# A mixture-of-experts stage on TensorE: which products share the four column tiles, and which engine turns the hidden activations

## The chip, the cores and the metric

One core of a Trainium2 chip runs the program. The metric is device time in microseconds (us), from launch to end, as the median of repeated executions; a profiled execution gives the trace. TensorE is called PE below, its weight loads PEld, VectorE DVE, ScalarE ACT, and SP is the queue that issues the transfers.

## What is computed

A sequence of 256 tokens of width 1024, in fp32, goes through a convolution layer with a dense feed-forward part, a sliding-window attention layer with a mixture of experts, two hybrid layers and a last norm. The change touches the mixture alone:

```python
def moe_swiglu(h, router, we_gate, we_up, we_down):
    logits = (h @ router).astype(jnp.float32)
    top_v, top_i = lax.top_k(logits, TOP_K)
    top_w = jax.nn.softmax(top_v, axis=-1)
    gates = jnp.sum(jax.nn.one_hot(top_i, N_EXPERTS) * top_w[..., None], axis=-2)
    out = jnp.zeros_like(h)
    for e in range(N_EXPERTS):
        out = out + gates[..., e:e + 1] * swiglu(h, we_gate[e], we_up[e], we_down[e])
    return out
```

There are 8 experts and each token goes to 2 of them. An expert has two matrices of 1024 x 3584 (gate and up) and one of 3584 x 1024 (down), 44 MB in fp32, 352 MB for all eight.

## The kernel before

**Slots.** Each expert works on its own tokens only. They are gathered into 96 slots (`CAP`), three blocks of 32 (blocks 0 to 2). `prepare` (L1404) makes ready two experts at a time: `onehot` (L1321) builds the token-to-slot matrix on DVE, `gather` (L1334) multiplies the normed tokens with it (32 matmuls), and `back` (L1354) turns it for the way back. `back` makes, for one expert, 6 transposes of 128x128 on PE, 6 products of 128x1 (the gate of every slot), each of which appears as two instructions, and masked copies on ACT. Were an expert to have more than 96 tokens, a second pass would run (L1315); it does not run in this execution.

**Products.** A matmul whose stationary operand has 32 columns fills one of four column tiles of the array, and its result goes to 32 partitions of a PSUM bank; four such matmuls, one per tile, run at the same time (`four`, L1417). An fp32 matmul appears as two instructions in the trace. The stationary operand is a block of 32 slots, the moving one 256 columns of weights. The hidden width of 3584 is cut into 14 chunks of 256. In `proj` (L1422) tiles 0 to 2 hold the three slot blocks and stream the same chunk of weights; tile 3 takes one of the blocks with another chunk, so that four chunks make three steps. An expert has 9 such steps and one for its last two chunks. The four matmuls of a group thus stream two different pieces of weights. The down products (`down`, L1477) do the same with four column parts of the down weights.

**Between the two products.** `act` (L1447) makes silu(gate) * up on ACT and DVE, 128 partitions x 256. `turn` (L1465) transposes it on PE, two transposes of 128x128 (four of 96x96 in the last step), into a PSUM bank, from which DVE copies it. `finish` (L1488) calls `turn`, then the down products. The loop (L1506) issues the projections of step n and then finishes step n-1, so the transposes stand between two runs of expert products on PE.

**Way back.** After an expert's last step `scatter` (L1380) splits its three partial outputs into a high and a low part, scaled by the slots' gates (ACT, then DVE), and multiplies them with the turned one-hot matrices (24 matmuls of 128x256 in all, as the fourth column part is spread over the blocks); DVE adds the result into `xT`, the running residual.

**Order.** All calls are recorded and a planner (`Recorder.issue`, L541) lays out a fixed order for each engine and assigns buffers, by estimated costs; an instruction that would wait in the plan lets a later one pass. All instructions therefore carry one line in the trace, L685. Weight tiles of 512 KB go to `large` buffers (35, at most 33 for raw weights) by transfers on SP, in the order of the program, each as soon as a buffer is free: 84 per expert. PSUM has 8 banks. `MEM_AT` and `GATHER_AT` (L44, L45) say before or after which step two other pieces of work go in: the memory keys and values of the second hybrid layer (`mem_second`), at step 22 of 80, and `prepare` for the next two experts, after the fourth step of every second expert. After the mixture the kernel reads a count into a register and branches (L1314 to L1316), and the next layer begins.

Of the kernel before, what the change touches and what calls it, by code (L numbers as in the profile page):

```python
# [30 lines left out]
NC4 = 3  # L31
# [12 lines left out]
MEM_AT = 2, 122  # L44
GATHER_AT = 1, 0  # L45
# [38 lines left out]
def _ch(w):  # L84

    return w.reshape(2, 4, 128, w.shape[1] // 256, 256).transpose(3, 2, 0, 1, 4)
# [49 lines left out]
def _consts():  # L136
# [37 lines left out]
    add("slot", np.broadcast_to((np.arange(2 * CAP) % CAP)[None, :] - BIG, (128, 2 * CAP)))  # L174
    add("part", np.concatenate([p < CAP, p >= CAP], 1))
# [16 lines left out]
def layout(i):  # L192
# [21 lines left out]
        "e_gate": np.stack([_ch(w) for w in i["sw_we_gate"][0]]),  # L214
        "e_up": np.stack([_ch(w) for w in i["sw_we_up"][0]]),
        "e_down": np.stack([_dn(w) for w in i["sw_we_down"][0]]),
# [471 lines left out]
class Net:  # L688
# [632 lines left out]
    def onehot(self, e, base):  # L1321

        nc = self.nc
        both = [self.t([128, 2, 2 * CAP], F32R, "onehot") for _ in range(2)]
        for j in range(2):
            for i in range(2):
                at = self.pos[:, j, e + i:e + i + 1]
                if base:
                    nc.vector.tensor_scalar(both[j][:, i], self.C("slot"), base, at, op0=OP.add, op1=OP.is_equal)
                else:  # L1330
                    nc.vector.tensor_scalar(both[j][:, i], self.C("slot"), at, None, op0=OP.is_equal)
        return both

    def gather(self, oh):  # L1334
        nc = self.nc
        G = [[], []]
        for c in range(4):
# [4 lines left out]
            for i in range(2):  # L1342
                at = (2 * c + i) % 4 * 128
                for n in range(4):
                    part, j = n // 2, n % 2
                    nc.tensor.matmul(pv[:, i], self.xn[j][part][c // 2][:, at:at + 128], oh[j][:, :, :CAP],
                                     start=n == 0 and i == 0, stop=n == 3, skip_group_check=True)
# [6 lines left out]
    def back(self, oh, x, e):  # L1354

        nc = self.nc
        pa, pb = self.acc("pmt"), self.acc("pmt")
        for v in range(3):
            p, at = (pa, v * S) if v < 2 else (pb, 0)
            for j in range(2):  # L1360
                nc.tensor.transpose(p[:, at + j * 128:at + (j + 1) * 128], oh[j][:, x, 32 * v:32 * v + 128].bitcast(F32),
                                    self.C("ident"))
        for v in range(3):
            for j in range(2):
                nc.tensor.matmul(pb[:, S + v:S + v + 1], oh[j][:, x, 32 * v:32 * v + 128].bitcast(F32),
                                 self.gate[:, j, e:e + 1], start=j == 0, stop=j == 1, skip_group_check=True)
        T = []
        low, high = self.C("part", 0, 1), self.C("part", 1, 1)
        two = [self.t([128, 2, S], F32R, "ohT") for _ in range(2)]
        for t, m in zip(two, (low, high)):  # L1370
            nc.scalar.activation(t.rearrange("p a s -> p (a s)"), pa, AF.Copy, scale=m)
        one = self.t([128, 2, S], F32R, "ohT")
        for n, m in enumerate((low, high)):
            nc.scalar.activation(one[:, n], pb[:, :S], AF.Copy, scale=m)
        gs = self.sm(3, "gs")
        nc.vector.tensor_copy(gs, pb[:, S:S + 3])
        T = [(two[0][:, 0], two[1][:, 0]), (two[0][:, 1], two[1][:, 1]), (one[:, 0], one[:, 1])]
        return T, gs

    def scatter(self, back, y):  # L1380
        nc = self.nc
        T, gs = back
        ys = []
        for v in range(3):
            h = self.t([128, S], F32R, "yh")
            l = self.t([128, S], F32R, "yl")
            self.split(h, l, y[v], scale=gs[:, v:v + 1])
            ys.append((h, l))
        for mp in range(4):
            p = self.acc("psc")  # L1390
            todo = [(v, part) for v in ([mp] if mp < 3 else range(3)) for part in range(2)]
            for i in range(2):
                for n, (v, part) in enumerate(todo):
                    nc.tensor.matmul(p[:, i * S:(i + 1) * S], ys[v][part][:, i * 128:(i + 1) * 128], T[v][mp == 3],
                                     start=n == 0 and i == 0, stop=n == len(todo) - 1, skip_group_check=True)
            nc.vector.tensor_tensor(self.xT[mp], self.xT[mp], p.rearrange("p (a s) -> p a s", a=2), op=OP.add)

    def experts(self, base=0.0):
        nc, a = self.nc, self.a
        steps = [(e, q, v) for e in range(NE) for q in range(NC4) for v in range(3)]  # L1400
        steps = [s for e in range(NE) for s in [x for x in steps if x[0] == e] + [(e, NC4, 0)]]
        G, B, Y, H, T, D = {}, {}, {}, {}, {}, {}
# [8 lines left out]
        def chunk(name, e, c):  # L1411
            return self.load_raw(a[name][e, c])

        def rows(e, k, b):
            return G[e][k][:, 32 * b:32 * b + 32]

        def four(outs, x, w, start, stop):  # L1417

            for j in range(4):
                nc.tensor.matmul(outs[j], x[j], w[j], start=start, stop=stop, skip_group_check=True)  # L1420

        def proj(s):  # L1422
            e, q, v = s
            p = self.mm()
            quarter = lambda p, at: [p[32 * j:32 * j + 32, at:at + 256] for j in range(4)]
            if q < NC4:
                if v == 0:
                    D[e, q] = [chunk(n, e, 4 * q + 3) for n in ("e_gate", "e_up")]
                mine = [chunk(n, e, 4 * q + v) for n in ("e_gate", "e_up")]
                for k in range(KT):  # L1430
                    u, i = k // 4, k % 4
                    x = [rows(e, k, j if j < 3 else v) for j in range(4)]
                    for m in range(2):
                        ws = [mine[m][u][:, i]] * 3 + [D[e, q][m][u][:, i]]
                        four(quarter(p, m * 256), x, ws, k == 0 and m == 0, k == KT - 1)
                return p
            last = [chunk(n, e, c) for n, c in (("e_up", 13), ("e_gate", 12), ("e_up", 12), ("e_gate", 13))]
            p2 = self.mm()
            for m in range(3):
                out = quarter(p if m < 2 else p2, m % 2 * 256)  # L1440
                for k in range(KT):
                    u, i = k // 4, k % 4
                    x = [rows(e, k, j if j < 3 else m) for j in range(4)]
                    four(out, x, [last[1 + m][u][:, i]] * 3 + [last[0][u][:, i]], k == 0 and m != 1, k == KT - 1)
            return p, p2

        def act(s, p):  # L1447
            e, q, v = s
            if q < NC4:
                g = self.t([128, 256], F32, "eg")  # L1450
                nc.scalar.activation(g, p[:, :256], AF.Silu)
                nc.vector.tensor_tensor(g, p[:, 256:], g, op=OP.mult)
                H[s] = [g]
                return
            p, p2 = p
            g, h = self.t([128, 256], F32, "eg"), self.t([128, 256], F32, "eg")
            nc.scalar.activation(g[:CAP], p[:CAP, :256], AF.Silu)
            nc.vector.tensor_tensor(g[:CAP], p[:CAP, 256:], g[:CAP], op=OP.mult)
            nc.scalar.activation(h[:CAP], p2[:CAP, :256], AF.Silu)
            for b, up in enumerate((p[96:, :256], p[96:, 256:], p2[96:, :256])):  # L1460
                r = slice(32 * b, 32 * b + 32)
                nc.vector.tensor_tensor(h[r], up, h[r], op=OP.mult)
            H[s] = [g, h]

        def turn(s):  # L1465
            n = 128 if s[1] < NC4 else CAP
            hs = H.pop(s)
            pt = self.acc("pht")
            t = self.t([128, 2 * len(hs), n], F32, "eh")
            pv = pt[:, :2 * len(hs) * n].rearrange("p (a b) -> p a b", b=n)  # L1470
            for x, g in enumerate(hs):
                for i in range(2):
                    nc.tensor.transpose(pv[:, 2 * x + i], g[:n, i * 128:(i + 1) * 128], self.C("ident")[:n, :n])
            nc.vector.tensor_copy(t, pv)
            T[s] = t

        def down(e, c, cols):  # L1477
            if c == 0:
                y = [self.acc("y0"), self.acc("y1")]
                Y[e] = [y[0][:, :256], y[0][:, 256:], y[1][:, :256]]  # L1480
            for i, w in enumerate(self.load_raw(a["e_down"][e, c])):
                for v in range(3):
# [250 lines left out]
```

## Time and profile before

| what | value |
|---|---|
| median of 3 runs | 2251.2 us (2250.46 to 2252.23) |
| profiled execution | 2245.66 us |
| its span | 2243.8 us |
| mean granted clock of TensorE | 0.987 |
| moved by DMA | 556.93 MB, mean 248 GB/s |

The span is what the trace covers; the profiled execution's time is 1.9 us longer. The trace gives, for any stretch of the span, each engine's busy time, its instructions in order of time, who waited for whom, and the rate of the DMA engines. Matmul ends are modelled, so where matmuls follow one another the pace is read from the starts.

### The profile page before, as it was taken

To read this page: it belongs to the slowest core of one execution; us is meant where nothing else is said; L and a number is where in the kernel's file an instruction comes from. 1 tells how busy PE (TensorE), PEld (TensorE's weight loads), DVE (VectorE), ACT (ScalarE), POOL (GpSimd) and SP (SyncE) were. 2 spreads that over 40 slices of the span, in tenths; PEclk is the share of its full clock that TensorE was granted. 3 is DMA by queue.
4 is the path that set the end of the run, shared out by engine and by line. 5 is a ranking of instruction groups with operands and counts; after the bars stand their busy time and mean duration, and the time that the engine had idled before them with its cause. 6 is when DMAs were issued, how large, how long until landed. Compare 5 with 4: busy or idle time off the path is not lost. (4 is left out here: it accounts for less than half of the span.)

```text
span 2243.8 us, 58323 instructions
## 1 busy us (share of the span) xinstructions
PE 2197.1 (98%) x25832; PEld 1716.0 (76%) x25832; DVE 917.3 (41%) x1911; ACT 717.0 (32%) x1259; POOL 0.2 (0%) x4
## 2 busy tenths in 40 slices
PE   8999999999999999999999999899999999999998
PEld 8789997865656556555665555487999998799997
DVE  8976568401101010010101010275485566657554
ACT  9454457310100001000010000165454454545441
POOL 0000000000000000000000000000000000000000
PEclk9999999999999999999999999998999999999998
DMA  7345657389889998999989999282466555355550
GB/s 281 92 160 174 202 186 247 132 315 384 335 303 342 352 401 304 388 379 400 334 319 375 399 358 376 72 333 69 125 222 192 186 180 188 102 163 178 189 169 20
DMA packets 156221, 556.93 MB, mean 248 GB/s; under 512 B 17456, under 2 KB 20144, under 8 KB 155952
## 3 DMA queue, kind: packets, MB, share of 16 engines
q1 hardware_dynamic: 155952, 553.03, 69.2%
q8 instruction: 206, 3.38, 0.6%
q14 instruction: 63, 0.52, 0.1%
HBM read 551.92 MB, written 1.05 MB: 246 GB/s over the span
## 5 line engine op out<-in xcount | busy, mean ns | idle before, releaser
L685 PE MATMUL bank<-large,gen 128*32 128x256 f32 (+2 forms) x15092 | 1006.4, 379 | 11.3 <-ACT gen L685 8.8
L685 PE MATMUL bank<-gen,large 128*128 128x256 f32 x7524 | 931.8, 285 | 8.1 <-ACT large L685 7.2
L685 PEld LDWEIGHTS bank<-gen,large 128*128 128x128 f32 x7524 | 910.2, 189 | 23.5 <-ACT large L685 7.6
L685 PEld LDWEIGHTS bank<-large,gen 128*32 128x32 f32 (+1 forms) x15092 | 612.9, 115 | 350.6 <-ACT gen L685 10.3
L685 DVE TENSOR_TENSOR large<-large,large 128x1024 fp32r<-128x1024 f32 (+1 forms) x356 | 425.7, 1210 | 127.8 <-PE bank L685 68.8
L685 ACT ACTIVATE large<-large 128x1024 fp32r<-128x1024 f32 (+2 forms) x363 | 367.5, 1036 | 239.9 <-PE bank L685 87.9
L685 ACT ACTIVATE gen<-bank 128x256 f32<-128x256 f32 (+5 forms) x184 | 74.2, 424 | 705.0 <-PE bank L685 687.5
L685 DVE COPY gen<-bank 128x256 f32<-128x256 f32 (+3 forms) x74 | 33.0, 446 | 600.5 <-PE bank L685 600.4
L685 PE MATMUL bank<-large,large 128*32 128x256 f32 (+1 forms) x1964 | 139.4, 384 | 0.0
L685 ACT ACTIVATE gen<-gen 128x512 f32<-128x512 f32 (+3 forms) x139 | 83.2, 610 | 157.3 <-DVE gen L685 156.3
L685 DVE TENSOR_TENSOR gen<-bank,gen 128x256 f32<-128x256 f32 (+4 forms) x150 | 75.0, 503 | 128.7 <-ACT gen L685 74.5
L685 PEld LDWEIGHTS bank<-large,large 128*32 128x32 f32 (+1 forms) x1964 | 73.7, 113 | 46.3 <-issue 4.4
L685 DVE TENSOR_TENSOR gen<-gen,gen 128x512 f32<-128x512 f32 (+3 forms) x126 | 79.1, 636 | 49.6 <-ACT gen L685 48.3
L685 PEld LDWEIGHTS bank<-ct,gen 128*128 128x128 f32 (+2 forms) x488 | 58.4, 157 | 52.4 <-issue 27.4
L685 PE MATMUL bank<-ct,gen 128*128 128x128 f32 (+3 forms) x488 | 86.8, 285 | 10.7 <-DVE gen L685 9.2
L685 PE MATMUL bank<-gen,gen 128*64 128x256 f32 (+5 forms) x520 | 83.7, 354 | 0.9 <-ACT gen L685 0.9
L685 ACT ACTIVATE gen<-bank,small 128x256 f32<-128x256 f32 (+3 forms) x88 | 46.6, 558 | 106.4 <-PE bank L685 94.8
L685 ACT ACTIVATE large<-bank 128x256 f32<-128x256 f32 (+2 forms) x26 | 9.5, 375 | 203.5 <-PE bank L685 193.9
L685 PEld LDWEIGHTS bank<-gen,gen 128*64 128x64 f32 (+2 forms) x520 | 52.8, 176 | 23.0 <-issue 8.3
L685 DVE TENSOR_TENSOR xT<-xT,bank 128x512 f32<-128x512 f32 x64 | 42.2, 685 | 31.5 <-PE bank L685 31.4
L685 DVE SCALAR_TENSOR_TENSOR gen<-bank,gen 128x256 f32<-128x256 f32 (+1 forms) x65 | 24.7, 424 | 56.1 <-PE bank L685 52.5
L685 DVE SCALAR_TENSOR_TENSOR gen<-gen,pt,gen 128x256 f32<-128x256 f32 x108 | 43.3, 484 | 1.3 <-ACT gen L685 1.2
(83 smaller groups left out, 514.8 us busy)
## 6 DMA issues: line engine op xcount, KB each, us to landing
large<-e_gate SPq DMA_DIRECT2D x224, 512.0 KB, 8.1
large<-e_up SPq DMA_DIRECT2D x224, 512.0 KB, 7.7
large<-e_down SPq DMA_DIRECT2D x224, 512.0 KB, 7.8
large<-c_up SPq DMA_DIRECT2D x64, 512.0 KB, 4.6
large<-c_dn SPq DMA_DIRECT2D x64, 512.0 KB, 4.9
large<-c_g SPq DMA_DIRECT2D x48, 512.0 KB, 4.5
large<-c_qk SPq DMA_DIRECT2D x24, 512.0 KB, 5.0
large<-cv_gate SPq DMA_DIRECT2D x22, 512.0 KB, 5.2
```

What stands on the lines that cost most here:

```text
L685: op.fn(*[real(x) for x in op.args], **{k: real(x) for k, x in op.kw.items()})
```

## The change

One slot block is put in all four column tiles, and each tile streams a different quarter of a weight tile. An expert now has 4 groups instead of 10 steps: three of 1024 hidden columns and one of 512. In each group all three blocks are done from the same weight tiles, in three PSUM banks. With this layout the activations [4 x 32 slots, 256 columns] become the stationary operand of the down product by 32x32 transposes, which DVE makes; the rows of the down weights are reordered to match. The PE transposes, their PSUM bank and the DVE copies go. `back` makes 2 transposes and one product of ones with a diagonal (the gate of every token, on all partitions) instead of 6 and 6, and `scatter` first moves the 12 parts of 32x256 to their place (6 copies on ACT, 6 on DVE), splits two tiles instead of three, makes 16 matmuls instead of 24, and multiplies by the gate on DVE before each of the four adds. The number of expert products, of weight tiles and of bytes stays. `mem_second` now goes in before group 8 of 32 (before: step 22 of 80), `prepare` after the second group of every second expert.

```diff
-GATHER_AT = 1, 0
+GATHER_AT = 1
-MEM_AT = 2, 122
+MEM_AT = 2, 108
+def _gu(gate, up):
+    main = [w[:, :3072].reshape(8, 128, 3, 1024).transpose(2, 0, 1, 3) for w in (gate, up)]
+    tail = [w[:, 3072:].reshape(8, 128, 4, 128) for w in (gate, up)]
+    return np.concatenate([np.stack(main, 2).reshape(48, 128, 1024), np.stack(tail, 3).reshape(8, 128, 1024)])
+def _gd(w):
+    main = w[:3072].reshape(3, 4, 8, 32, D).transpose(0, 2, 1, 3, 4).reshape(24, 128, D)
+    return np.concatenate([main, w[3072:].reshape(4, 4, 32, D).transpose(1, 0, 2, 3).reshape(4, 128, D)])
...
     def back(self, oh, x, e):
+        p = self.acc("pmt")
+        for j in range(2):
+            nc.tensor.transpose(p[:CAP, j * 128:(j + 1) * 128], oh[:, j, x].bitcast(F32), self.C("ident"))
+        dg = self.t([128, S], F32, "dg")
+        for j in range(2):
+            nc.vector.tensor_scalar(dg[:, j * 128:(j + 1) * 128], self.C("ident"), self.gate[:, j, e:e + 1], None,
+                                    op0=OP.mult)
+        nc.tensor.matmul(p[:, S:], self.C("ones"), dg, start=True, stop=True)
+        T = self.t([128, S], F32R, "ohT")[:CAP]
+        nc.scalar.activation(T, p[:CAP, :S], AF.Copy)
+        gb = self.t([128, S], F32, "gb")
+        nc.scalar.activation(gb, p[:, S:], AF.Copy)
...
     def scatter(self, back, y):
+        yn = [self.t([128, 512], F32, "yn") for _ in range(2)]
+        for j in range(4):
+            for b in range(BLOCKS):
+                o = yn[j // 2][32 * b:32 * b + 32, j % 2 * 256:j % 2 * 256 + 256]
+                i = y[b][32 * j:32 * j + 32]
+                if (j + b) % 2:
+                    nc.scalar.activation(o, i, AF.Copy)
+                else:
+                    nc.vector.tensor_copy(o, i)
+        for n in range(2):
+            h, l = self.t([128, 512], F32R, "yh")[:CAP], self.t([128, 512], F32R, "yl")[:CAP]
+            self.split(h, l, yn[n][:CAP])
...
             for i in range(2):
+                at = mp % 2 * 256 + i * 128
+                for part in range(2):
+                    nc.tensor.matmul(p[:, i * S:(i + 1) * S], ys[mp // 2][part][:, at:at + 128], T,
+                                     start=part == 0 and i == 0, stop=part == 1, skip_group_check=True)
+            t = self.t([128, 2, S], F32, "gy")
+            nc.vector.tensor_tensor(t, p.rearrange("p (a s) -> p a s", a=2), gbb, op=OP.mult)
+            nc.vector.tensor_tensor(self.xT[mp], self.xT[mp], t, op=OP.add)
...
     def experts(self, base=0.0):
+        def four(out, at, x, w, start, stop):
             for j in range(4):
+                nc.tensor.matmul(out[32 * j:32 * j + 32, at:at + 256], x, w[:, 256 * j:256 * j + 256], start=start,
+                                 stop=stop, skip_group_check=True)
         def proj(s):
+            e, g = s
+            p = [self.mm() for _ in range(BLOCKS)]
+            for k in range(KT):
+                at = [48 + k] if g == GROUPS - 1 else [(g * KT + k) * 2, (g * KT + k) * 2 + 1]
+                ws = [self.tile_of(a["e_in"][e, n]) for n in at]
+                for b in range(BLOCKS):
+                    for m, w in enumerate(ws):
+                        four(p[b], m * 256, G[e][k][:, 32 * b:32 * b + 32], w, k == 0 and m == 0, k == KT - 1)
+            return p
         def act(s, p):
+            for b in range(BLOCKS):
+                g = self.t([128, 256], F32, "eg")[:, :w]
+                nc.scalar.activation(g, p[b][:, :w], AF.Silu)
+                nc.vector.tensor_tensor(g, p[b][:, w:2 * w], g, op=OP.mult)
+                t = self.t([128, 256], F32, "eh")
+                nc.vector.transpose(t[:, :w], g)
+                T[s].append(t)
+        def down(s):
+            for c in range(n):
+                w = self.tile_of(a["e_down"][e, 8 * g + c])
+                for b in range(BLOCKS):
+                    four(Y[e][b], b % 2 * 256, t[b][:, 32 * c:32 * c + 32], w, g == 0 and c == 0 and b != 1,
+                         g == GROUPS - 1 and c == n - 1)
...
             act(s, proj(s))
             if n:
-                finish(steps[n - 1])
+                down(steps[n - 1])
+            if s[1] == GATHER_AT and s[0] % 2 and s[0] + 1 < NE:
+                prepare(s[0] + 1)
```

## Rows read from the trace of the kernel before

**Rows 1.** Busy time by stretch: us, PE, PEld, DVE, ACT, POOL, PEclk, DMA share, GB/s.

```profile
453.00:1443.50 990.50, 988.11 (x16746) 592.08 (x16738) 110.96 (x268) 72.24 (x178) 0.00 (x0) 1.00 0.92 346
...
530.00:570.00 40.00, 40.00 (x718) 23.39 (x711) 4.62 (x11) 1.91 (x5) 0.00 (x0) 1.00 1.03 413
```

**Rows 2.** Groups of PE instructions, 453 to 1443.5 us: xcount, busy us, mean ns, idle before.

```profile
L685 PE MATMUL bank<-large,gen 128*32 128x256 f32 x14208 | 807.9, 380 | 2.4 <-DVE gen L685 2.4
L685 PE MATMUL bank<-large,large 128*32 128x256 f32 x1920 | 126.4, 384 | 0.0
```

**Rows 3.** Timeline of PE, expert products and the transposes between: start us, us, instruction, xcount.

```profile
921.31 6.25 PE L685 MATMUL bank<-large,large 128*32 128x256 f32 x112
927.37 3.64 PE L685 MATMUL bank<-large,gen 128*32 128x256 f32 x64
...
1254.30 9.70 PE L685 MATMUL bank<-large,gen 128*32 128x256 f32 x176
1263.93 0.44 PE L685 MATMUL bank<-ct,gen 128*128 128x128 f32 x2
1264.30 9.86 PE L685 MATMUL bank<-large,gen 128*32 128x256 f32 x176
```

**Rows 4.** Who waited for PE and SP, 453 to 1443.5 us: us in total, times, longest.

```profile
PE bank L685 <- DVE gen L685: 2.4, 5, 0.7
...
SPq L685 <- PE bank L685: 598.1, 419, 9.4
```

**Rows 5.** Timeline of PE, the end of one prepare, and a product with a diagonal.

```profile
614.97 0.82 PE L685 MATMUL bank<-ct,gen 128*128 128x128 f32 x6
615.62 1.40 PE L685 MATMUL bank<-small,gen 128*128 128x1 f32 x12
616.88 0.85 PE L685 MATMUL bank<-ct,gen 128*128 128x128 f32 x6
...
618.90 5.39 PE L685 MATMUL bank<-large,gen 128*32 128x256 f32 x96
...
430.65 0.60 PE L685 MATMUL bank<-gen,ct 128*128 128x256 f32 x2
431.08 1.89 PE L685 MATMUL bank<-gen,large 128*128 128x256 f32 x8
```

**Rows 6.** Timeline of PE within one expert's scatter.

```profile
578.02 0.64 PE L685 MATMUL bank<-large,large 128*128 128x256 f32 x4
578.50 0.40 PE L685 MATMUL bank<-large,gen 128*128 128x256 f32 x2
```

**Rows 7.** Timeline of all engines at the end of the mixture.

```profile
1443.13 1.20 ACT L685 ACTIVATE gen<-bank,small 128x256 fp32r<-128x256 f32 x3 [9.89 <-PE bank L685]
1443.65 3.62 PE L685 MATMUL bank<-large,gen 128*128 128x256 f32 x24 [0.16 <-ACT gen L685]
...
1447.31 0.69 DVE L685 TENSOR_TENSOR xT<-xT,bank 128x512 f32<-128x512 f32 x1 [0.23 <-PE bank L685]
```

**Rows 8.** Groups of DVE instructions, 453 to 1443.5 us.

```profile
L685 DVE TENSOR_TENSOR gen<-bank,gen 128x256 f32<-128x256 f32 x55 | 22.9, 417 | 27.5 <-ACT gen L685 27.4
L685 DVE TENSOR_TENSOR xT<-xT,bank 128x512 f32<-128x512 f32 x28 | 18.0, 684 | 9.1 <-PE bank L685 9.1
L685 DVE TENSOR_TENSOR gen<-bank,gen 32x256 f32<-32x256 f32 x24 | 10.2, 427 | 0.5
...
L685 DVE TENSOR_TENSOR large<-large,large 128x1024 fp32r<-128x1024 f32 x2 | 2.4, 1222 | 0.0
```

**Rows 9.** Timeline of PE in a hybrid layer's attention, two column tiles of 64.

```profile
1927.40 1.99 PE L685 MATMUL bank<-gen,gen 128*64 128x256 f32 x16 [0.86 <-ACT gen L685]
1929.32 0.66 PE L685 MATMUL bank<-ct,large 128*128 128x128 f32 x4
...
1931.38 0.87 PE L685 MATMUL bank<-gen,gen 128*64 128x256 f32 x8
1932.19 0.33 PE L685 MATMUL bank<-ct,gen 128*128 128x128 f32 x1
```

More of the change, by code (lines that the diff above doesn't have):

```diff
@@ L30 @@
 CAP = 96
-NC4 = 3
+BLOCKS = CAP // 32
+GROUPS = 4
 RMS_EPS = 1e-6
@@ L173, in _consts @@
     add("before", (p < j))
-    add("slot", np.broadcast_to((np.arange(2 * CAP) % CAP)[None, :] - BIG, (128, 2 * CAP)))
-    add("part", np.concatenate([p < CAP, p >= CAP], 1))
+    add("slot", np.broadcast_to(np.arange(CAP)[None, :] - BIG, (128, CAP)))
     e = np.arange(NE)
@@ L213, in layout @@
         "sw_out": _ws(np.concatenate([sw_out[perm], sw_out[CC:]], 0)),
-        "e_gate": np.stack([_ch(w) for w in i["sw_we_gate"][0]]),
-        "e_up": np.stack([_ch(w) for w in i["sw_we_up"][0]]),
-        "e_down": np.stack([_dn(w) for w in i["sw_we_down"][0]]),
+        "e_in": np.stack([_gu(g, u) for g, u in zip(i["sw_we_gate"][0], i["sw_we_up"][0])]),
+        "e_down": np.stack([_gd(w) for w in i["sw_we_down"][0]]),
     }
@@ L1323, in onehot @@
         nc = self.nc
-        both = [self.t([128, 2, 2 * CAP], F32R, "onehot") for _ in range(2)]
+        t = self.t([128, 2, 2, CAP], F32R, "onehot")
         for j in range(2):
@@ L1328, in onehot @@
                 if base:
-                    nc.vector.tensor_scalar(both[j][:, i], self.C("slot"), base, at, op0=OP.add, op1=OP.is_equal)
+                    nc.vector.tensor_scalar(t[:, j, i], self.C("slot"), base, at, op0=OP.add, op1=OP.is_equal)
                 else:
-                    nc.vector.tensor_scalar(both[j][:, i], self.C("slot"), at, None, op0=OP.is_equal)
-        return both
+                    nc.vector.tensor_scalar(t[:, j, i], self.C("slot"), at, None, op0=OP.is_equal)
+        return t
     def gather(self, oh):
@@ L1356, in back @@
         nc = self.nc
[L1357 to L1376, printed above, removed]
@@ L1390, in scatter, with tile_of @@
             p = self.acc("psc")
-            todo = [(v, part) for v in ([mp] if mp < 3 else range(3)) for part in range(2)]
             for i in range(2):
[L1393 to L1396, printed above, removed]
+                at = mp % 2 * 256 + i * 128
[5 more added lines that the diff above has]
+            nc.vector.tensor_tensor(self.xT[mp], self.xT[mp], t, op=OP.add)
+    def tile_of(self, src):
+        nc = self.nc
+        nc.bias = -LOAD_FIRST - nc.shift * (1 - LOAD_SHIFT)
+        t = nc.tile("raw", list(src.shape))
+        nc.sync.dma_start(t, src)
+        nc.bias = 0
+        return t
     def experts(self, base=0.0):
         nc, a = self.nc, self.a
-        steps = [(e, q, v) for e in range(NE) for q in range(NC4) for v in range(3)]
-        steps = [s for e in range(NE) for s in [x for x in steps if x[0] == e] + [(e, NC4, 0)]]
-        G, B, Y, H, T, D = {}, {}, {}, {}, {}, {}
+        steps = [(e, g) for e in range(NE) for g in range(GROUPS)]
+        G, B, Y, T = {}, {}, {}, {}
         def prepare(e):
@@ L1422, in proj @@
         def proj(s):
[L1423 to L1444, printed above, removed]
@@ L1465, in turn @@
[L1465 to L1475, printed above, removed]
@@ L1477, in down @@
-        def down(e, c, cols):
-            if c == 0:
-                y = [self.acc("y0"), self.acc("y1")]
-                Y[e] = [y[0][:, :256], y[0][:, 256:], y[1][:, :256]]
-            for i, w in enumerate(self.load_raw(a["e_down"][e, c])):
-                for v in range(3):
-                    x = [cols[(v + j) % 3][:, i] for j in range(4)]
-                    ws = [w[:, 0, n * 256:(n + 1) * 256] for n in (v, v, v, 3)]
-                    outs = [Y[e][v][32 * j:32 * j + 32] for j in range(4)]
-                    four(outs, x, ws, c == 0 and i == 0 and v != 1, c == 13 and i == 1)
@@ new lines, in down @@
+        def down(s):
+            e, g = s
+            if g == 0:
+                y = [self.acc("y0"), self.acc("y1")]
+                Y[e] = [y[0], y[0], y[1]]
+            n = 4 if g == GROUPS - 1 else 8
+            t = T.pop(s)
+            for c in range(n):
[3 more added lines that the diff above has]
+                         g == GROUPS - 1 and c == n - 1)
+            if g == GROUPS - 1:
+                y = Y.pop(e)
+                self.scatter(B.pop(e), [y[b][:, b % 2 * 256:b % 2 * 256 + 256] for b in range(BLOCKS)])
@@ L1510, in experts @@
             if n:
-                finish(steps[n - 1])
-            e, q, v = s
-            if (q, v) == GATHER_AT and e % 2 and e + 1 < NE:
-                prepare(e + 1)
-        finish(steps[-1])
+                down(steps[n - 1])
+            if s[1] == GATHER_AT and s[0] % 2 and s[0] + 1 < NE:
+                prepare(s[0] + 1)
+        down(steps[-1])
     def fill(self, at):
```

52 lines of the change are left out of this document (6 added, 46 removed).

## The prediction

> **What bounds the kernel now.** I read the busy times by stretch first. The expert products run from 453 to 1443.5 us, 990.5 of the 2243.8 us of the span, and in that stretch PE is busy 988 us while DVE and ACT are busy 111 and 72 us [rows 1]; the reader is to see that only PE can set the pace here, unless the transfers do. Outside the stretch the change touches little, so all else is taken as it is.
>
> The groups of PE instructions say what PE does there: 14208 + 1920 = 16128 instructions on column tiles of 32 [rows 2]. Their busy times overlap, four at a time, so the price is read from the starts in the timeline: 112 of them lie between 921.31 and 927.37 us, 54.1 ns each, that is 216.4 ns for four side by side [rows 3]. At that pace 16128 take 872.5 us. The other 118 us of the stretch are what stands between them, and there the change works.
>
> The waits come last. PE waited 2.4 us in all for DVE and is not listed as waiting for a transfer; SP waited 598 us for PE to give a weight buffer back [rows 4]. So the transfers run ahead and are held by the buffers.
>
> **The change, part by part.** *Expert products.* Their number stays: an expert had 9 x 64 + 96 projections and 28 x 12 down products, 1008, and has 3 x 192 + 96 and 28 x 12 after. With two instructions for each and 8 experts this is the 16128 counted. I price them as before, 872.5 us; what could be wrong is that four tiles now stream four different pieces of weights where they streamed two. That is bounded at the end of this part.
>
> *PE transposes go.* After 1254.30 us, 176 products at 54.1 ns end at 1263.82; the next run starts at 1264.30 [rows 3]. A pair of transposes thus costs 0.48 us, most of it not the transposes but the way into the full array and back. There are 9 steps x 8 experts = 72 pairs, and 8 last steps with four smaller ones, which I price as a pair: 80 x 0.48 = 38.4 us. The 2.4 us in which PE waited for DVE go too, as DVE's copies out of the transposes' bank were what it could wait for. Sum: -40.8 us. What is late next is the DVE transpose. It is not in the trace; the nearest rows are a DVE product from PSUM of 128x256 at 0.42 us and one of 128x1024 at 1.22 us [rows 8], and I take 0.42 by the equal shape. 96 of them are 40 to 117 us of DVE, which is busy 111 of 990 us. None is on PE's path: the down products of a group wait until the projections of the next one are done, and the last group of all still has the down products of the group before it in front, 8 tiles x 24 instructions x 54.1 ns = 10.4 us, against 3 x (0.42 + 1.22) = 4.9 us on DVE at the dear end. If that cover were gone, each of 32 groups would show up to 4.9 us.
>
> *Back.* For a pair of experts, 12 transposes and 24 instructions of 128x1 take PE from 614.97 to 618.90, 3.93 us [rows 5]. After, there are 4 transposes, at (615.62 - 614.97) / 6 = 0.11 us each, and two products with a diagonal, at 431.08 - 430.65 = 0.43 us each: 1.3 us. Four pairs save 4 x 2.6 = -10.4 us. The first lies before the stretch, but PE is not idle there either.
>
> *Scatter.* 24 matmuls become 16. Four of them start within 578.50 - 578.02 = 0.48 us, 0.12 us each [rows 6]. Seven experts x 8 x 0.12 = -6.7 us; the eighth is part of the end.
>
> *The end.* After the last product the scatter is in the open. Now it takes from 1443.13 to 1447.31 + 0.69 = 1448.00, 4.9 us [rows 7]. After, DVE has a chain: 6 copies of 32x256 at 0.427, two splits at 0.684 and four times multiply and add at 0.684 each, 2.6 + 1.4 + 5.5 = 9.4 us, with some 0.5 us of waits [rows 8]. That is +5 us. If the copies cost half it is +4, and if each step waits for ACT or PE as well, +8. In the other seven experts the same chain lies beside 100 us of products.
>
> *Order and queues.* SP issues as many transfers of the same size, in the order of use. `prepare` moves from two fifths of an expert to one half, `mem_second` from a little inside the third expert to its start; neither adds an instruction. What the planner makes of it is not known: gathers, scatters and `mem_second` may be cut into more pieces between the products. One visit to the full array costs 0.48 - 2 x 0.11 = 0.26 us beyond its work [rows 3, 5]. I take 16 more visits, 2 per expert, +4 us; bounds are none, 0, and 100 more, +26 us.
>
> *Four pieces of weights.* The nearest rows are attention products on two tiles of 64 columns, each streaming its own data: 8 in 0.81 us and 16 in 1.92 us, at most 0.240 us for two side by side, against 0.2164 us [rows 9]. So the loss lies between nothing and 11%, 96 us, on 872.5 us. A gain is excluded, as each tile must still take its 256 columns. I take nothing, since the shorter row shows 0.203 us for its pairs and both rows have a change of mode at their ends.
>
> *Transfers.* The stretch moved 346 GB/s x 990.5 us = 342.7 MB; shortened by the 51 us that the terms above take from it, it needs 365 GB/s. With PE at its usual pace 413 GB/s came in for 40 us [rows 1], and SP's 598 us of waiting [rows 4] say that more was to be had. I take no loss.
>
> **Sum.** -40.8 - 10.4 - 6.7 + 5 + 4 = -48.9 us. Against the profiled execution's own 2245.66 us this is 2196.8 us. The median of the runs is 2251.2 us, 5.5 us above that execution, so in its terms I forecast 2202 us.
>
> **The rivals.** *Loads become the bound.* In the trace the mean of the stretch is 346 GB/s, and the need is 365. If the queue held no more than half way between, 356 GB/s, the stretch could not be under 342.7 MB / 356 = 963 us, 28 us less than now; with the end's +5 the time is 2228 us. For it speaks that the mean is this near; against it the 413 GB/s row and SP's waits. A rule of the Trainium skill makes the same point: the page "DMA: Bandwidth & Descriptors", section "Where 436 GB/s comes from", has the HBM side of a load bind at about 358 GB/s per core. By that figure the stretch would be 957 us and the time 2223 us. This trace does not agree with it as a ceiling, with its 413 GB/s.
>
> *Four pieces cost.* This is the one that ends slower. Each group of four products takes longer because its tiles fetch from four places; the gain of 49 us is used up when a group takes 216.4 x (1 + 48.9 / 872.5) = 228.5 ns, 12 ns more. At the upper row's 11% the time is 2202 + 96 = 2298 us. For it speaks the 0.240 us row alone, whose length includes a change of mode; against it that two different pieces cost nothing visible in the groups of now.
>
> *Banks.* The products hold two PSUM banks for the down sums and three for each of two groups, all eight. If gathers and scatters push a group's third bank back, PE waits for ACT and DVE. At the dear 4.9 us per group and 32 groups that is 157 us, 2359 us. Against it: between two groups' projections lie the down products, 10.4 us, in which the banks come free.
>
> *More pieces.* The change does what it says, but with 100 more visits: 2202 + 22 = 2224 us.
>
> *It does less than it says.* If the pair of transposes were hidden beside the products, the removed 38 us would not show. The starts exclude it: 1264.30 is 0.48 us after the last product's due time.
>
> **How the numbers follow.** My forecast, 2186 to 2212, has 0.72; loads 0.10; more pieces 0.06; four pieces that cost 0.06; banks 0.03; and 0.03 that the time falls under 2186, where neither the visits nor the end cost anything and more waits go. The range from 2186 to 2228 takes in the forecast, the additional visits and the loads as priced, and leaves about 0.15 out. Faster by over 0.2%, about what a measurement of this kernel can tell from no change, are the forecast, the visits, the faster case and most of the loads: 0.90. Slower are the four pieces and most of the banks, 0.08; 0.02 is left for no difference.
>
> **What would show it.** In the trace after: no products with the 128x128 identity between runs of expert products, apart from 2 per expert from `back`; 32 groups; the stretch of expert products at about 940 us, with the loads at about 365 GB/s; PE's starts still 216 ns apart for four; DVE transposes near 0.4 us, and nobody waiting for them; some 10 us from the last product to the last add on `xT`. I am wrong if four products take 228 ns or more, if PE is listed as waiting for transfers of `e_in` or `e_down` or for ACT's and DVE's bank releases, or if the visits to the full array number over 100.

## The result and the profile after

The kernel after takes 2193.71 us (median of 4 runs, 2192.22 to 2195.86) against 2251.72 us (2250.46 to 2252.36) for the kernel before beside it: ratio 0.9744, with the interval 0.9727 to 0.9761. Its profiled execution took 2192.56 us, with a span of 2190.8 us and a mean granted clock of 0.985. The two profiled executions are 53.1 us apart, the two medians 58.0 us. To find the 53 us in the span, cut both spans at the first expert product, at the last one and at the first matmul of the next layer:

| part of the span | before, us | after, us | difference | forecast |
|---|---|---|---|---|
| to the first expert product | 452.7 | 446.3 | -6.3 | -2.6 |
| the stretch of expert products | 990.4 | 937.0 | -53.5 | -51.3 |
| from the last product to the next layer | 12.8 | 20.0 | +7.2 | +5 |
| the rest | 787.9 | 787.4 | -0.4 | 0 |

Busy time by stretch, kernel after (columns as in [rows 1]):

```profile
446.30:1383.30 937.00, 927.05 (x16430) 577.04 (x16430) 141.34 (x341) 76.80 (x204) 0.00 (x0) 1.00 0.94 364
...
700.00:840.00 140.00, 136.89 (x2476) 82.93 (x2472) 30.62 (x70) 12.45 (x31) 0.00 (x0) 1.00 1.00 390
980.00:1060.00 80.00, 79.41 (x1441) 45.95 (x1434) 10.01 (x26) 6.65 (x17) 0.00 (x0) 1.00 1.02 406
```

PE is still the engine that sets the pace, though it now idles 10 us of the stretch, where it idled 2.4 before. The loads ran at 364 GB/s over the whole stretch, where 365 were forecast as needed, and at 390 and 406 GB/s for 140 and 80 us.

Groups of instructions by form, kernel after, 446.3 to 1383.3 us (PE answers to [rows 2], DVE to [rows 8]):

```profile
L693 PE MATMUL bank<-large,gen 128*32 128x256 f32 x11871 | 670.6, 380 | 0.0
...
L693 PE MATMUL bank<-large,large 128*32 128x256 f32 x4256 | 254.2, 379 | 0.0
...
L693 DVE STREAM_TRANSPOSE gen<-gen 128x256 f32<-128x256 f32 x34 | 14.7, 440 | 0.9
...
L693 DVE STREAM_TRANSPOSE gen<-gen 128x128 f32<-128x128 f32 x20 | 6.2, 312 | 0.9
```

The number of products is that of before; the 128x128 transposes between them are gone, and DVE makes one of 128x256 in 0.44 us.

Waits in the stretch, kernel after (answers to [rows 4]):

```profile
PE bank L693 <- ACT gen L693: 8.4, 6, 1.6
...
PE bank L693 <- ACT large L693: 1.6, 1, 1.6
...
SPq L693 <- PE bank L693: 482.2, 383, 6.9
```

PE waits for no transfer and not for the DVE transposes; SP still waits 482 us for buffers (598 before). New are seven waits of PE for ACT, 10.0 us together. The timeline of PE shows where one of them is, and the shape of scatter and `prepare` now (answers to [rows 3, 5, 6]):

```profile
575.87 2.34 PE L693 MATMUL bank<-large,gen 128*32 128x256 f32 x40
579.77 0.50 PE L693 MATMUL bank<-gen,large 96*128 96x256 f32 x2 [1.56 <-ACT large L693]
580.20 0.64 PE L693 MATMUL bank<-large,gen 128*32 128x256 f32 x8
580.77 1.94 PE L693 MATMUL bank<-gen,large 96*128 96x256 f32 x14
582.63 1.72 PE L693 MATMUL bank<-large,gen 128*32 128x256 f32 x28
...
611.26 3.82 PE L693 MATMUL bank<-gen,gen 128*128 128x192 f32 x32
614.92 0.38 PE L693 MATMUL bank<-ct,gen 128*96 128x128 f32 x2
615.14 0.60 PE L693 MATMUL bank<-large,ct 128*128 128x256 f32 x2
615.57 0.38 PE L693 MATMUL bank<-ct,gen 128*96 128x128 f32 x2
615.79 0.60 PE L693 MATMUL bank<-large,ct 128*128 128x256 f32 x2
616.32 1.93 PE L693 MATMUL bank<-large,gen 128*32 128x256 f32 x32
```

Read the starts: the products end at 578.2 us, the first two of the scatter's matmuls start at 579.77, because ACT's split is not there yet; 8 product instructions slip in; then come the other 14. The two `back`s lie between 614.92 and 616.32, 1.4 us, where 1.3 were forecast (3.9 before).

In the same way every break in the run of expert products can be measured, from the start of the last product before it to the start of the next one, less the 0.196 us that lie between two sets of four starts in an unbroken run. Before there were 108 such visits of PE to other work, 107.4 us together; after there are 29, 63.4 us. By kind, with what the visits of before's scatter cost by taking groups of four matmuls apart (below) put to the scatter:

| in the stretch | before, us | after, us | difference | forecast |
|---|---|---|---|---|
| transposes and the wait for DVE | 42.8 | 0 | -42.8 | -40.8 |
| three `prepare`s | 23.2 | 18.7 | -4.5 | -7.8 |
| seven scatters | 35.3 | 29.7 | -5.6 | -6.7 |
| `mem_second` | 15.0 | 15.0 | 0 | 0 |
| more visits | | | | +4 |
| products, beyond 872.5 us | 1.6 | 1.1 | -0.5 | 0 |

The end of the mixture, timeline of all engines, kernel after (answers to [rows 7]):

```profile
1383.30 0.37 ACT L693 ACTIVATE gen<-bank 32x256 f32<-32x256 f32 x1 [14.83 <-PE bank L693]
1383.70 0.41 DVE L693 COPY gen<-bank 32x256 f32<-32x256 f32 x1 [14.38 <-ACT gen L693]
...
1384.43 1.04 ACT L693 ACTIVATE large<-large 128x1024 fp32r<-128x1024 f32 x1
1384.56 1.75 DVE L693 COPY gen<-bank 32x256 f32<-32x256 f32 x4 [0.44 <-ACT gen L693]
1386.34 1.23 DVE L693 TENSOR_TENSOR large<-large,large 128x1024 fp32r<-128x1024 f32 x1
...
1389.76 3.88 PE L693 MATMUL bank<-gen,gen 96*128 96x256 f32 x16 [6.06 <-ACT gen L693]
...
1395.40 1.28 DVE L693 TENSOR_TENSOR xT<-xT,gen 128x512 f32<-128x512 f32 x2
...
1403.35 6.96 PE L693 MATMUL bank<-large,gen 128*128 128x512 f32 x22 [9.71 <-ACT gen L693]
```

The last add ends at 1396.68, 13.4 us after the last product (4.9 before; about 10 forecast). The copies take until 1389.1: they alternate between ACT and DVE, and both engines put splits of the next layer's weights (1.04 and 1.23 us each) in between.

A cost that no term of the forecast has is TensorE's clock. In the stretches of time below the granted clock was 0.5, the lower of its two levels (1.2 of 2.4 GHz). The first two rows are of the kernel before, the others of the kernel after (columns as in [rows 1]):

```profile
442.70:446.20 3.50, 3.50 (x12) 2.96 (x12) 1.31 (x4) 1.77 (x4) 0.00 (x0) 0.51 0.00 0
879.60:883.10 3.50, 3.50 (x37) 1.66 (x41) 0.16 (x1) 1.36 (x3) 0.00 (x0) 0.51 0.50 150
...
946.00:949.40 3.40, 3.40 (x26) 2.38 (x28) 3.40 (x6) 0.00 (x0) 0.00 (x0) 0.50 1.04 414
...
1386.30:1406.80 20.50, 7.33 (x24) 6.34 (x25) 12.39 (x22) 7.73 (x17) 0.00 (x0) 0.50 0.16 48
```

At 879.6 us, behind `mem_second`, four product instructions of before took 0.43 us instead of 0.22; these are its 1.6 us beyond 872.5. After, the fourth and the sixth scatter met such a drop (at 946.0 and at 1181.5 us) shortly after PE had waited 1.6 us for ACT's splits. Each cost 0.8 us more than the others, and the products behind it about 0.7 us; four other scatters had PE waiting as long without a drop. At the end PE had been idle since 1383.7 us, and its 16 matmuls start 0.21 us apart, where they do so 0.12 us apart in the stretch.

### The profile page after: what moved, and what is told of

Read it like the earlier page. It is cut to its first block, busy times and chain, and to the rows that moved or that the text cites. A ratio compares the mean times of both kernels' runs of the same rounds, so it can differ in the third digit from the quotient of the medians.

```text
span 2190.8 us, 57629 instructions
## 1 busy us (share of the span) xinstructions
PE 2132.2 (97%) x25480; PEld 1697.7 (77%) x25480; DVE 958.1 (44%) x1999; ACT 725.3 (33%) x1291; POOL 0.2 (0%) x4
## 5 line engine op out<-in xcount | busy, mean ns | idle before, releaser
L693 PE MATMUL bank<-gen,large 128*128 128x256 f32 (+1 forms) x7528 | 934.6, 286 | 10.3 <-ACT large L693 9.4
L693 PEld LDWEIGHTS bank<-gen,large 128*128 128x128 f32 (+1 forms) x7528 | 911.7, 189 | 26.8 <-ACT large L693 10.3
L693 PE MATMUL bank<-large,gen 128*32 128x256 f32 (+2 forms) x12672 | 853.3, 380 | 14.4 <-ACT gen L693 14.4
L693 DVE TENSOR_TENSOR large<-large,large 128x1024 fp32r<-128x1024 f32 (+2 forms) x357 | 426.7, 1207 | 101.8 <-PE bank L693 77.3
L693 ACT ACTIVATE gen<-bank 128x256 f32<-128x256 f32 (+7 forms) x236 | 91.1, 404 | 725.5 <-PE bank L693 712.0
L693 PE MATMUL bank<-large,large 128*32 128x256 f32 (+1 forms) x4328 | 272.0, 379 | 0.0
L693 PEld LDWEIGHTS bank<-large,large 128*32 128x32 f32 (+1 forms) x4328 | 158.8, 112 | 91.8 <-ACT large L693 0.4
L693 ACT ACTIVATE gen<-gen 128x512 f32<-128x512 f32 (+4 forms) x148 | 89.3, 612 | 172.9 <-DVE gen L693 171.6
L693 DVE TENSOR_TENSOR gen<-gen,gen 128x512 f32<-128x512 f32 (+4 forms) x128 | 80.7, 639 | 50.6 <-ACT gen L693 48.9
L693 PE MATMUL bank<-gen,gen 64*128 64x256 f32 (+5 forms) x508 | 84.8, 356 | 10.2 <-ACT gen L693 10.2
```

Source lines behind the costliest of these rows:

```text
L693: op.fn(*[real(x) for x in op.args], **{k: real(x) for k, x in op.kw.items()})
```

## The experiments

The theory: the gain is the time that PE lost in going to the transposes and back, since PE has no slack in the stretch; the new layout of the products and its loads cost nothing, and the new copies before the scatter are what is late now. Ratios are to the kernel before on the same chip.

**The transposes alone.** The kernel before, with the transposes in `turn` made by DVE:

```diff
-                for i in range(2):
-                    nc.tensor.transpose(pv[:, 2 * x + i], g[:n, i * 128:(i + 1) * 128], self.C("ident")[:n, :n])
-            nc.vector.tensor_copy(t, pv)
+                nc.vector.transpose(t[:n, 2 * x:2 * x + 2].rearrange("p a b -> p (a b)"), g[:n, :2 * n])
+                if n == CAP:
+                    nc.vector.tensor_copy(t[CAP:, 2 * x:2 * x + 2].rearrange("p a b -> p (a b)"), g[64:CAP, :2 * n])
```

The down weights keep their old order of rows, so its down products pair activations and weights in another order than the reference.

> The kernel before, with only the PE transposes of the hidden activations replaced by 32x32 transposes on DVE (the rows of the down product are then not matched to it, so the output is not the reference's; in the last step 32 rows are filled by a copy). Tiles, weights, back and scatter stay as before. My theory, that the transposes' 80 visits to the full array carry most of the gain: 40 to 45 us less than before, 2207 to 2212 us, with the stretch of expert products near 948 us. Rival, that the gain comes from the new arrangement of weight tiles and loads: within 10 us of before, 2242 us or more.

Measured: 2200.03 us (2196.82 to 2203.01), ratio 0.9772 (0.9736 to 0.9809), 7 us under the range that was expected: the medians are 52.6 us apart, the two profiled executions 44.4. Busy time by stretch of this kernel:

```profile
456.40:1397.80 941.40, 941.40 (x16571) 583.00 (x16570) 123.91 (x292) 71.74 (x178) 0.00 (x0) 1.00 0.94 364
```

The stretch is 941.4 us, 49.1 less than before, with the old groups, gathers and scatters, and it loads at the same 364 GB/s. 42.4 us of it are visits (27 are left, 65.0 us), the other 6.7 us lie inside the runs of products. So most of the gain needs neither the new layout of the products nor the new way back, and a bound by the loads at the forecast's rate is not there. The time to the first product is 456.4 us, 3.7 later than before, in layers that this edit does not touch. There the granted clock of this run was 0.50 from 374.8 to 388.5 us, where that of before was 1.00; PE had waited 1.6 us for DVE just ahead of it. Half of these 13.7 us, 6.9, is the most that this can have cost.

**The visits put back.** The kernel after, with a pair of 128x128 transposes of a constant before each block of each group, 96 pairs, into the bank that the block's first product then overwrites:

```diff
                 for b in range(BLOCKS):
+                    if k == 0:
+                        for i in range(2):
+                            nc.tensor.transpose(p[b][:, i * 128:(i + 1) * 128], self.C("ident"), self.C("ident"))
```

> The kernel after, with two identity transposes put on PE ahead of each block's first product of every group (96 pairs, into the block's own bank, which the first product then overwrites; the result is unchanged). My theory: up to 96 visits to the full array at 0.48 to 0.6 us, so 46 to 58 us more than after, 2240 to 2252 us, less where the plan puts the pairs of a group together (32 visits of six transposes, 0.26 + 0.66 us each, 29 us, 2223 us). Rival, that PE has slack in the stretch because the loads set its pace (364 GB/s): under 10 us more, below 2204 us.

Measured: 2231.42 us (2230.65 to 2232.51), ratio 0.9913 (0.9878 to 0.9947); the stretch is 974.8 us, 37.8 more than after. Timeline of PE of this kernel:

```profile
914.12 0.44 PE L693 MATMUL bank<-ct 128*128 128x128 f32 x2
914.49 0.64 PE L693 MATMUL bank<-large,large 128*32 128x256 f32 x8
915.05 0.44 PE L693 MATMUL bank<-ct 128*128 128x128 f32 x2
915.42 0.64 PE L693 MATMUL bank<-large,large 128*32 128x256 f32 x8
```

From 914.49 to 915.42 are 0.93 us for 8 product instructions and a pair; 8 x 54.1 ns are 0.43, so the pair costs 0.50 us here. 80 of the pairs stand alone, at a mean of 0.48 us, 38.5 us; 4 more came apart into 8 visits of a single transpose, 3.0 us; 11 fell in with visits that are there anyway, and one lies before the first product. The price per pair is that of the forecast, [rows 3], and PE hides nothing of it. The total lies between the two that were expected (2240 to 2252 us, and 2223 us with the pairs of a group together), because fewer pairs stand alone and because PE's waits for ACT fell by 3.2 us, to 6.8.

**Copies dealt by bank.** In the kernel after, ACT and DVE take turns within each of the two PSUM banks that hold an expert's partial outputs (blocks 0 and 1 share the first). Here ACT takes the first bank and DVE the second, 8 and 4 copies instead of 6 and 6:

```diff
-                if (j + b) % 2:
+                if b < 2:
```

> The kernel after, with scatter's 12 copies dealt by PSUM bank: the 8 from the first bank on ACT, the 4 from the second on DVE. In the trace of after the copies of ACT and DVE take turns, 4.3 us for 12 instead of 2.6 for 6 beside 6. If it is the bank that makes them take turns, they now run beside one another, 8 x 0.38 = 3.1 us, PE's waits of 1.6 us in seven scatters shrink to about 0.4 and the end is 1 us shorter: 6 to 12 us less than after, 2182 to 2188 us. If it is the output tile, they still take turns and the time stays within 4 us of 2194.

**Copies dealt by target.** As a rival, dealt by the tile that they write, so that each engine has its own target but both still touch both banks:

```diff
-                if (j + b) % 2:
+                if j < 2:
```

> The kernel after, with scatter's 12 copies dealt by output tile: the 6 into the first tile on ACT, the 6 into the second on DVE. If it is the output tile that makes ACT and DVE take turns, both run at once, 2.6 us, PE's waits in scatter go and the first tile is ready after 2.3 us: 8 to 14 us less than after, 2180 to 2186 us. If it is the PSUM bank, which both still read, they take turns as before and the time stays within 4 us of 2194.

Measured, on the same chip: by bank 2185.90 us (2184.96 to 2187.38), ratio 0.9714 (0.968 to 0.9748); by target 2192.47 us (2191.54 to 2194.41), ratio 0.9743 (0.9709 to 0.9777), as after. The timeline of all engines shows the copies of one expert, first in the kernel after:

```profile
575.69 0.37 ACT L693 ACTIVATE gen<-bank 32x256 f32<-32x256 f32 x1 [4.36 <-PE bank L693]
...
576.10 0.41 DVE L693 COPY gen<-bank 32x256 f32<-32x256 f32 x1 [3.83 <-ACT gen L693]
576.55 0.77 ACT L693 ACTIVATE gen<-bank 32x256 f32<-32x256 f32 x2 [0.48 <-DVE gen L693]
576.95 0.86 DVE L693 COPY gen<-bank 32x256 f32<-32x256 f32 x2 [0.44 <-ACT gen L693]
```

and dealt by bank:

```profile
575.65 1.53 ACT L693 ACTIVATE gen<-bank 32x256 f32<-32x256 f32 x4 [4.37 <-PE bank L693]
...
576.08 0.85 DVE L693 COPY gen<-bank 32x256 f32<-32x256 f32 x2 [3.86 <-PE bank L693]
576.96 0.86 DVE L693 COPY large<-bank 32x256 f32<-32x256 f32 x2
577.20 1.54 ACT L693 ACTIVATE large<-bank 32x256 f32<-32x256 f32 x4
```

The releaser in brackets is what to read. After, each engine waits for the other's copy, 0.4 to 0.5 us at a time, and the 12 copies take 4.3 us; dealt by bank they wait for PE alone, run side by side and take 3.1 us. Dealt by target the brackets name the other engine again:

```profile
576.82 1.24 ACT L693 ACTIVATE gen<-bank 32x256 f32<-32x256 f32 x3 [0.49 <-DVE large L693]
577.23 1.33 DVE L693 COPY large<-bank 32x256 f32<-32x256 f32 x3 [0.44 <-ACT gen L693]
```

So it is the bank that makes them take turns. Dealt by bank, PE's waits for ACT fall from 10.0 to 3.4 us, and the stretch to 928.8 us, 8.1 less than after. 6.6 of the 8.1 us are these waits. In the rest two things are mixed: no scatter of this kernel met the lower clock, but more groups of four are taken apart, since 6 product instructions slip in instead of 8.

**The gate back on the slots.** The copies by bank, and the gate no longer on the way back over the tokens but on the slots, as a scale of the split, as in the kernel before; the four DVE multiplies on the 128x512 results and the product with the diagonal go:

```diff
-        dg = self.t([128, S], F32, "dg")
...
-        nc.tensor.matmul(p[:, S:], self.C("ones"), dg, start=True, stop=True)
+            nc.tensor.matmul(p[:CAP, S:S + 1], oh[:, j, x].bitcast(F32), self.gate[:, j, e:e + 1], start=j == 0,
+                             stop=j == 1, skip_group_check=True)
...
-            self.split(h, l, yn[n][:CAP])
+            self.split(h, l, yn[n][:CAP], scale=gb)
...
-            nc.vector.tensor_tensor(t, p.rearrange("p (a s) -> p a s", a=2), gbb, op=OP.mult)
-            nc.vector.tensor_tensor(self.xT[mp], self.xT[mp], t, op=OP.add)
+            nc.vector.tensor_tensor(self.xT[mp], self.xT[mp], p.rearrange("p (a s) -> p a s", a=2), op=OP.add)
```

> The kernel with the copies dealt by bank (e3), and the gate applied per slot in the split, as in the kernel before, instead of per token by four DVE products of 128x512 after the matmuls. If DVE's chain sets the end of the mixture, as I put it, those four products of 0.68 us go from the open end: 2 to 4 us less than e3's 2185.9, 2182 to 2184 us, and from the last expert product to the last add some 10 us instead of 12.9. If the end is set by ACT's copies and the splits of the next layer's weights, within 1 us of e3.

Measured: 2180.74 us (2179.32 to 2181.40), ratio 0.9674 (0.9648 to 0.9699): the lowest ratio of all kernels here. Timeline of all engines at its end:

```profile
1372.31 0.76 ACT L693 ACTIVATE gen<-bank 32x256 f32<-32x256 f32 x2 [14.83 <-PE bank L693]
1372.74 1.74 DVE L693 COPY gen<-bank 32x256 f32<-32x256 f32 x4 [14.41 <-PE bank L693]
...
1378.38 3.97 PE L693 MATMUL bank<-gen,gen 96*128 96x256 f32 x16 [5.68 <-ACT gen L693]
...
1382.39 0.69 DVE L693 TENSOR_TENSOR xT<-xT,bank 128x512 f32<-128x512 f32 x1 [0.17 <-PE bank L693]
```

The last add ends 10.8 us after the last product instead of 12.9 with the copies by bank alone; it waits for PE, whose 16 matmuls ran at a granted clock of 0.5 here too. But the end is the smaller part of the gain. The span is 5.7 us shorter than with the copies by bank alone; 1.1 of them lie between the last product and the next layer, and 3.3 in the stretch, which is 925.5 us in 18 visits, 52.5 us together. There the plan leaves the third `prepare` in one piece (4.1 us), while PE's waits for ACT go from 3.4 to 4.9 us. The way from the last product to the next layer is 18.4 us, still 5.6 more than before: the copies and the splits of the next layer's weights are in it.

**The scatter's matmuls later.** In the last kernel two of the scatter's 16 matmuls still start early and 6 product instructions slip in before the other 14. Here the planner ranks those matmuls behind other work, so that they might start together:

```diff
+SCATTER_LATE = 4e3
...
+            nc.bias = SCATTER_LATE
...
+            nc.bias = 0
```

> e5 with scatter's matmuls given a later place in the plan by 4 us of PE work, so that more expert products stand between the end of an expert and its scatter. If PE's waits for the splits (3.4 us in all in e3) and the cut of scatter into two visits are what is left of scatter's price, 3 to 8 us less than e5, and the waits of PE in the stretch under 1 us. If they are not, within 2 us of e5.

Measured: 2210.30 us (2206.33 to 2212.30), ratio 0.9801 (0.9775 to 0.9828), 29.6 us slower than the kernel that it starts from: a miss. Timeline of its PE:

```profile
580.53 0.38 PE L694 MATMUL bank<-gen,gen 96*128 96x256 f32 x1
580.84 0.62 PE L694 MATMUL bank<-large,gen 128*32 128x256 f32 x2
581.39 0.39 PE L694 MATMUL bank<-gen,large 96*128 96x256 f32 x1
...
582.42 0.62 PE L694 MATMUL bank<-large,gen 128*32 128x256 f32 x2
582.97 0.38 PE L694 MATMUL bank<-gen,gen 96*128 96x256 f32 x1
```

A rank is not a date. The plan put one of the scatter's matmuls and two product instructions in turn, and the visits went from 18 to 65: 66.8 us instead of 52.5. Worse, the two are one matmul of a group of four, alone on its column tile: they take from 580.84 to 581.39, 0.55 us, as long as all four matmuls, 8 instructions, take between two pairs of transposes (914.49 to 915.05 us in the kernel with the visits put back). The 45 lone matmuls add 14.8 us. The visits, 14.3 us more than in the kernel that it starts from, and the products between them, some 14 us more, are the 28.3 us by which the stretch grew. PE's waits for ACT meanwhile stayed small (4.5 us), so the waits that this edit aimed at were the smaller cost.

**Half the buffers.** The kernel after with 16 buffers for raw weights instead of 33, to see whether the loads have room:

```diff
-N_RAW = 33
+N_RAW = 16
```

> The kernel after with at most 16 raw weight tiles in flight or in use instead of 33. If the loads have slack at the pace of after (364 GB/s asked, 390 to 406 seen over 80 to 140 us), the stretch of expert products stays within 10 us of 937 us, as 16 tiles still cover 20 us; the stages before and after may pay a few us of their own. If the loads are near their bound and the deep queue is what carries the stretch, it grows by more than 20 us, to 957 us or more, with PE waiting for transfers.

Measured: 2199.22 us (2198.18 to 2200.50), ratio 0.9754 (0.9724 to 0.9784); the kernel after has 0.9744, within this interval. The waits of its PE in the stretch:

```profile
PE bank L693 <- ACT gen L693: 9.0, 6, 1.6
...
PE bank L693 <- ACT large L693: 1.6, 1, 1.6
```

As after, no transfer is among them. The stretch is 943.2 us, 6.3 more; its visits are 48 instead of 29 and take 69.2 us, 5.8 more, since one `prepare` is cut into single gathers between runs of 24 products. The products beyond their pace are 1.6 us, which is all that late loads could have cost. So half the buffers would do for the loads, and what moved was the plan.

## Why the prediction was right

**The median.** 2193.7 us lies in the range and 8.3 under the forecast of 2202. Half of that is the sum: -53.1 us between the profiled executions where -48.9 was forecast. The other half is its base: the profiled execution of before was 5.5 us under its median, that of after 1.2 us. That the sum came this near is in part luck: single terms missed by up to 4 us in both directions, as the following shows.

**Transposes, -40.8.** The mechanism holds: with the transposes alone gone, the stretch is 49.1 us shorter; put back, each lone pair costs 0.48 us. The term was a little small: 42.8 us went, the wait for DVE included. What the forecast did not have is that a visit can take a group of four matmuls apart, at 0.33 us for each matmul left alone. Each of before's seven scatters took one group apart into four, 9 us in all. The kernel with the transposes alone sent to DVE has 6.7 us less inside its runs of products: about 4 because its scatters leave two matmuls alone instead of four, and 1.7 because its clock did not drop in the stretch.

**Back, -10.4.** Its own work fell as forecast, from 3.9 to 1.4 us per pair. In the stretch three pairs gave 4.5 us, not 7.8, as the plan cut one `prepare` into 12 visits (8.3 us), where the other two take 5.2 us each.

**Scatter, -6.7.** It gave -5.6 us, and by another sum: 8 matmuls and nearly all the groups taken apart are gone, but PE waits 10.0 us for the splits behind the copies, and two scatters met the lower clock, 1.6 us. The forecast had put that chain beside 100 us of products. It was right that nothing later waits for it, but not that PE would go on meanwhile: the plan sets the scatter's first matmuls at a fixed place, earlier than ACT is done. For the most part that is because the copies take turns at the banks: where they do not, 3.4 of the 10.0 us are left.

**The end, +5.** It came to +7.2. The row of before gave the right durations, but the sum had ACT's and DVE's copies side by side and left out the splits of the next layer's weights that both engines do in between, and PE's matmuls at the lower clock; it is near the upper bound, +8, which was for waits at each step.

**More visits, +4.** This step failed. Leaving out the 77 visits for the transposes alone, before had 31 and after has 29, two fewer where 16 more were forecast. The forecast was right only in that one `prepare` was cut.

**Before the stretch, -2.6.** It came to -6.3. 2.0 of them lie between the first add into the residual of the attention layer and the first product, 45.8 us before and 43.8 after, but they are not what was forecast. `back` did get some 2.6 us shorter there, yet the plan put ten more 128x256 matmul instructions of other work, 0.22 us each, ahead of the first product. And before had a granted clock of 0.51 from 442.7 to 446.2 us: the kernel with the transposes alone, with the `back` of before and without that drop, takes 44.2 us for the same way. The other 4.3 us arise in the attention layer, whose first add into the residual came at 402.6 instead of 406.8 us, though the change does not touch it. All the kernels built on the one after start their products at 446.3 to 446.8 us, so it goes with the program. The planner ranks each instruction by the chain of work behind it, which the change makes shorter, and its order on PE differs from that of before from the first layer on; that this is the cause is argued, not shown.

**The rivals.** *Four pieces cost*: no. A run of 2440 product instructions took 131.7 us, 54.0 ns each, as before [rows 3]; all products together are 1.1 us over that pace. *Loads become the bound*: no. The stretch loaded at 364 GB/s, above the 356 on which that rival's time rests, with half the buffers PE still waited for no transfer, and SP waited 482 us. By the page "DMA: Bandwidth & Descriptors" of the Trainium skill, section "Where 436 GB/s comes from", the HBM side binds at about 358 GB/s; 364 GB/s over 937 us and 406 over 80 us on the one core that runs do not agree with that as a ceiling. *Banks*: the products never waited for one; PE's seven waits are the scatter's. *More pieces*: not in the change as made, but half the buffers and the later scatter show the mechanism, at 19 and 47 visits more.

## What to carry to other kernels

Where one engine is busy all through a stretch, price a visit to another kind of work by the starts around it, not by its own duration: here 0.48 us for a pair of transposes of 0.22, and 0.33 us more for each matmul that it leaves alone out of a group that runs side by side. Then count visits, before and after, since a planner may change their number more than the edit does. When work moves to engines with much idle time, look whether two of them touch the same PSUM bank, for a wait written in there makes a chain of what the busy times show as parallel. And read the granted clock of a stretch before you explain a few us there by the program.

## What the runs showed that was not expected

- **ACT and DVE take turns at a PSUM bank**, even when they read different 32 partitions of it, as they do dealt by target: 12 copies took 4.3 us after, 3.9 us dealt by target, and 3.1 us when no bank was shared. The brackets show a wait for the other engine, and each copy is as long as where no bank was shared (0.37 to 0.43 us), so the time goes into waits between the engines and not into slower copies. The Trainium skill, page "PSUM — Partial Sum Buffer", section "PSUM bank collisions raise a hardware error", says that two engines may use different quadrants (32 partitions) of one bank at once; no run here shows that, as the program keeps them apart by the whole bank.
- **A group of four taken apart is dear**: one matmul of it alone between two visits, two instructions, takes 0.55 us, all four together, 8 instructions, 0.56 us.
- **DVE's 32x32 transpose** of 128x256 in fp32 takes 0.44 us and of 128x128 0.31 us, near the 0.42 us taken from a product of that shape.
